# Softmax with a relative-position bias: the sixth row of chunk 0 loaded in sixteen uneven transfers, and a small bias load

## The chip, the cores and the metric

The kernel runs on one core of one Trainium2 chip. The metric is the device time of one execution in microseconds (us); the time given is the median of several runs. The core has five instruction engines (here VectorE = DVE, ScalarE = ACT, GpSimd = POOL and SyncE = SP are used) and 16 DMA engines that move data between HBM and the on-chip memory SBUF, which has 128 partitions. The trace of one profiled execution gives the start and length of each instruction and of each DMA packet.

## The reference

The input `logits` has the shape (2, 8, 2112, 2112) in float32, `rel_bias` (8, 33). To each row of logits a bias is added that depends on the head and on the clipped distance between the row's and the column's position, and a softmax is taken over the row.

```python
rel = pos[:, None] - pos[None, :]
rel_clipped = np.clip(rel, -max_rel, max_rel) + max_rel   # max_rel = 16
bias = rel_bias[:, rel_clipped].copy()
logits = logits + bias[None, :, :, :]
logits = logits - logits.max(axis=-1, keepdims=True)
exp = np.exp(logits)
return (exp / exp.sum(axis=-1, keepdims=True)).astype(np.float32)
```

285.5 MB are read and as many written.

## The kernel before

**Tiling.** The 2 x 8 x 2112 rows are divided among 128 partitions, 264 (`ROWS`) consecutive rows for each; 8 (`PB`) partitions make one head of one batch entry. A row is 2112 (`S`) floats, 8448 B. A chunk is R = 6 rows of every partition (6336 KB), N = 44 chunks in all, and four buffers `X[0]` to `X[3]` (`NBUF`) hold four chunks; STEP = 24 rows are one turn of the loops. Every chunk is loaded into a buffer, worked on there and stored from it.

**Engines.** For each chunk, DVE adds the bias and takes the negated maximum of each row (`add`, L166), ACT takes the exponential and its sum (`exps`, L175), DVE takes the reciprocal and multiplies (`scale`, L183 and L187). The bias of the rows lies as a strip `F`, which DVE copies once in 24 rows (`strip`, L160) out of a table `M` in PSUM. That table is made once ahead of the loop from `rel_bias` (L117 to L156): masks from two iotas of POOL, then the 33 values of the partition's own head picked from a copy of all 8 x 33 values (L131, L135), and then the table.

**Queues.** SP issues all loads and stores of logits and output, in program order. Ahead of its loop it issues chunk 0 as six transfers of one row each (L87 to L90; the first five count on the semaphore `pre`, the last on `ld[0]`), and then the loads of chunks 1 to 3 (L91, L92). In its loop it issues, in turn, the store of a finished chunk (which waits for the multiplies, semaphore `scaled`) and the load of the next chunk into a buffer whose store has landed (semaphore `st`). The last chunk is stored in two halves. The load of `rel_bias` is issued from ACT's queue (L97 to L100): it gives each of the 128 partitions a copy of all 264 values. DVE waits for it at L129, for five rows of chunk 0 at L190 (and then copies the first strip), and for the sixth row in the first `add`.

A transfer over all 128 partitions is divided among the 16 DMA engines, eight partitions for each, and each partition's piece is a packet.

Of the kernel before, what the change touches and what calls it, by code (L numbers as in the profile page):

```python
# [15 lines left out]
def kernel(  # L16
# [6 lines left out]
    nc = tc.nc  # L23
    P = 128
    B, H, S, S2 = logits.shape
    assert S == S2
    MR = 16
    W = 2 * MR + 1
    ROWS = B * H * S // P
    PB = S // ROWS  # L30
    assert ROWS * P == B * H * S and PB * ROWS == S and PB == H == 8
    R = 6
    NBUF = 4
# [4 lines left out]
    MW = S + ROWS - 1  # L38
    FW = S + STEP - 1
    BIG = 3.0e38  # L40

    io = ctx.enter_context(tc.tile_pool(name="io", bufs=1))
    X = [io.tile([P, R * S], FP32, tag=f"X{b}", name=f"X{b}") for b in range(NBUF)]
    F = io.tile([P, FW], FP32, tag="F", name="F")
    rbS = io.tile([P, W], FP32, tag="rbS", name="rbS")
# [3 lines left out]
    ip = io.tile([P, 3, PB], I32, tag="ip", name="ip")  # L49
# [3 lines left out]
    def view(t, offset, dims):  # L53

        return bass.AP(tensor=t.tensor, offset=t.offset + offset, ap=[[list(t.ap[0])[0], P]] + dims)

    def rows(t, j, n):

        return bass.AP(tensor=t.tensor, offset=t.offset + j * S, ap=[[ROWS * S, P], [1, n * S]])

    with tc.tile_critical(no_gpsimd_drain=True):
        ld = [nc.alloc_semaphore(f"ld{b}") for b in range(NBUF)]
# [3 lines left out]
        scaled = nc.alloc_semaphore("scaled")  # L66
        inv = nc.alloc_semaphore("inv")
        rb = nc.alloc_semaphore("rb")
        pre = nc.alloc_semaphore("pre")
        idx = nc.alloc_semaphore("idx")  # L70
        dve = nc.alloc_semaphore("dve")

        def take(eng, sem, n):
            eng.wait_ge(sem, n).then_inc(sem, -n)  # L74


        def load(j, b):
            nc.sync.dma_start(out=X[b][:, :], in_=rows(logits, j, R)).then_inc(ld[b], 16)
# [5 lines left out]
            ).then_inc(st[b], 16)  # L84


        for r in range(R):  # L87
            nc.sync.dma_start(
                out=X[0][:, r * S : (r + 1) * S], in_=rows(logits, r, 1)
            ).then_inc(ld[0] if r == R - 1 else pre, 16)  # L90
        for n in range(1, NBUF):  # L91
            load(n * R, n)  # L92

        rbB = view(F, 0, [[1, H * W]])
        nc.scalar.dma_start(  # L97
            out=rbB,
            in_=bass.AP(tensor=rel_bias.tensor, offset=rel_bias.offset, ap=[[0, P], [1, H * W]]),
        ).then_inc(rb, 16)  # L100
        nc.gpsimd.iota(ip[:, 0], pattern=[[0, PB]], base=0, channel_multiplier=1).then_inc(idx, 1)
        nc.gpsimd.iota(ip[:, 2], pattern=[[1, PB]], base=0, channel_multiplier=0).then_inc(idx, 1)  # L102

        v = nc.vector
        done = [0]

        def then(ins):
            done[0] += 1
            ins.then_inc(dve, 1)

        def settle():
            v.wait_ge(dve, done[0])

        SC = H * W
        mask = [F[:, SC + i * PB : SC + (i + 1) * PB] for i in range(9)]
        dp, dh, eq, hm, gt, le, lt, ra, rz = mask
        v.wait_ge(idx, 2)  # L117
        then(v.tensor_scalar(out=ip[:, 1], in0=ip[:, 0], scalar1=3, scalar2=7,  # L118
                             op0=ALU.logical_shift_right, op1=ALU.bitwise_and))
# [7 lines left out]
        for m, op in ((eq, ALU.is_equal), (gt, ALU.is_gt), (le, ALU.is_le), (lt, ALU.is_lt)):  # L127
# [4 lines left out]
            out=view(F, 0, [[W, H], [1, W]]), in0=view(F, 0, [[W, H], [1, W]]),  # L132
            in1=view(F, SC + 3 * PB, [[1, H], [0, W]]), op=ALU.mult))
        settle()
        then(v.tensor_reduce(out=rbS[:, :], in_=view(F, 0, [[1, W], [W, H]]),  # L135
                             axis=mybir.AxisListType.X, op=ALU.add))
        settle()
        low, high = rbS[:, W - 1 : W], rbS[:, 0:1]
        then(v.tensor_scalar(out=ra, in0=gt, scalar1=low, scalar2=None, op0=ALU.mult))  # L139
        then(v.tensor_scalar(out=rz, in0=gt, scalar1=low, scalar2=None, op0=ALU.mult))  # L140
        then(v.tensor_tensor(  # L141
            out=view(F, 0, [[W, PB], [1, W]]), in0=view(F, SC + 2 * PB, [[1, PB], [0, W]]),
            in1=view(rbS, W - 1, [[0, PB], [-1, W]]), op=ALU.mult))
# [6 lines left out]
            out=view(M, U, [[ROWS, PB], [1, W]]), in0=view(F, 0, [[W, PB], [1, W]]),  # L150
            in1=view(F, SC + 8 * PB, [[1, PB], [0, W]]), op=ALU.add))
        then(v.tensor_copy(out=view(M, U + W, [[ROWS, PB], [1, ROWS - W]]),  # L152
                           in_=view(F, SC + 7 * PB, [[1, PB], [0, ROWS - W]])))
        then(v.tensor_copy(out=M[:, 0:U], in_=low.to_broadcast([P, U])))  # L154
# [7 lines left out]
        def add(b):  # L162
            take(v, ld[b], 16)
            for r in range(b * R, (b + 1) * R):
                x = X[b][:, (r - b * R) * S : (r - b * R + 1) * S]
                v.tensor_tensor_reduce(  # L166
                    out=x, in0=x, in1=F[:, STEP - 1 - r : STEP - 1 - r + S], scale=-1.0, scalar=BIG,
                    op0=ALU.add, op1=ALU.min, accum_out=nmax[:, r : r + 1],
# [18 lines left out]
                    v.tensor_scalar_mul(out=x, in0=x, scalar1=rec[:, r : r + 1]).then_inc(scaled, 1)  # L187

        v.sem_inc(dve, -done[0])
        take(v, pre, 16 * (R - 1))  # L190
        with nc.Fori(0, ROWS - STEP + 1, STEP, engines=[ENG.DVE]) as j:  # L191
            strip(j)
            take(v, dve, 1)
# [51 lines left out]
```

## Time and profile before

| | |
|---|---|
| median of 3 runs | 1330.1 us (1329.99 to 1332.06) |
| span of the profiled execution, first to last instruction | 1327.7 us |
| DMA rate over the span | 430 GB/s |
| SP's DMA queue, share of 16 engines | 99.6% |
| busy: DVE, ACT, POOL | 74%, 43%, 0% |
| last multiply of DVE ends | 1303.6 us |

In the views of the profile, a row of the timeline gives start, length, engine, line, operation and tiles; in brackets stands how long the engine was idle before it and what ended that. `SPq` and `ACTq` are the instruction queues of SP and ACT, which issue DMAs. A row of the windows gives a stretch of time, its length, the busy time of DVE, ACT and POOL with the number of instructions, the clock of the matrix engine (which is not used here), the mean busy share of the 16 DMA engines and the rate in GB/s; a packet is counted whole in the window in which it starts, so a short window can show a share above 1. A row for a DMA queue gives packets, MB, and the share of the time of 16 engines.

### The profile page before, as it was taken

How to read it: one execution, taken by the hardware profiler on the slowest of the kernel's cores; microseconds unless marked ns; L12 is line 12 of the kernel's file. 1: busy time of each engine (PE TensorE's matmuls, PEld its weight loads, DVE VectorE, ACT ScalarE, POOL GpSimd, SP SyncE). 2: the span in 40 equal slices, each digit the busy share in tenths (PEclk: the TensorE clock that was granted, in tenths of full speed). 3: DMA queues.
4: the chain of work that ended last, by engine and by line, in shares of the span. 5: the costliest groups of instructions: out<-in, count | busy, mean ns of one | idle time of the engine just before them, and what ended most of it. 6: DMA issues, size and time to landing. Idle time of an engine off the chain costs nothing. (4 is left out here: it accounts for less than half of the span.)

```text
span 1327.7 us, 2454 instructions
## 1 busy us (share of the span) xinstructions
DVE 976.6 (74%) x911; ACT 575.2 (43%) x539; POOL 0.4 (0%) x6
## 2 busy tenths in 40 slices
DVE  6999667777777776687778777677877776687772
ACT  2564333444444343345444333444444343335440
POOL 0000000000000000000000000000000000000000
DMA  9999999999999999999999999999999999999998
GB/s 392 431 428 437 435 420 437 435 434 425 435 437 434 428 435 434 435 429 429 438 438 432 426 438 437 437 425 437 437 437 425 435 440 437 428 432 438 437 426 359
DMA packets 13683, 571.11 MB, mean 430 GB/s; under 512 B 1521, under 2 KB 1649, under 8 KB 1649
## 3 DMA queue, kind: packets, MB, share of 16 engines
q1 hardware_dynamic: 13536, 570.96, 99.6%
q10 hardware_dynamic: 144, 0.14, 0.1%
q14 instruction: 3, 0.02, 0.0%
HBM read 285.61 MB, written 285.47 MB: 430 GB/s over the span
## 5 line engine op out<-in xcount | busy, mean ns | idle before, releaser
L166 DVE CUSTOM_DVE_ANT_0 X<-X,F 128x2112 f32<-128x2112 f32 x264 | 605.2, 2354 | 301.3 <-DVEq L74 301.3
L175 ACT ACTIVATE X<-X,nmax 128x2112 f32<-128x2112 f32 x264 | 541.7, 2052 | 539.3 <-ACTq L74 517.6
L187 DVE TENSOR_SCALAR X<-X,rec 128x2112 f32<-128x2112 f32 x264 | 332.4, 1315 | 13.2
L175 ACT ACT_TABLE_LOAD x11 | 14.1, 1283 | 183.3 <-ACTq L74 183.3
L175 ACT ACTIVATION_READ_ACCUMULATOR X<-X,nmax 128x1 f32 x264 | 49.2, 186 | 0.0
L160 DVE COPY F<-M 128x2135 f32 x11 | 26.1, 2374 | 6.3 <-DVEq L74 6.3
L166 DVE DVE_READ_ACCUMULATOR2_ANT nmax<- 128x1 f32 x264 | 21.7, 82 | 0.0
L183 DVE RECIPROCAL rec<-tot 128x3 f32<-128x3 f32 x88 | 14.9, 170 | 0.0
L131 DVE TENSOR_TENSOR F<-F 128x264 f32<-128x264 f32 x1 | 0.4, 434 | 4.7 <-DMA F<-in_rel_bias_dram 4.7
L152 DVE COPY M<-F 128x1848 f32<-128x1848 f32 x1 | 2.1, 2077 | 0.0
L118 DVE TENSOR_SCALAR ip<-ip 128x8 int32<-128x8 int32 x1 | 0.2, 173 | 1.3 <-POOL ip L102 1.3
L135 DVE TENSOR_REDUCE rbS<-F 128x33 f32<-128x264 f32 x1 | 0.6, 610 | 0.0
L149 DVE TENSOR_TENSOR M<-F 128x264 f32<-128x264 f32 x1 | 0.4, 441 | 0.0
L141 DVE TENSOR_TENSOR F<-F,rbS 128x264 f32<-128x264 f32 x1 | 0.4, 425 | 0.0
L128 DVE TENSOR_SCALAR F<-F 128x8 f32<-128x8 f32 x4 | 0.4, 166 | 0.0
L154 DVE COPY M<-rbS 128x247 f32<-128x247 f32 x1 | 0.4, 408 | 0.0
L139 DVE TENSOR_SCALAR F<-F,rbS 128x8 f32<-128x8 f32 x1 | 0.2, 231 | 0.0
L145 DVE SCALAR_TENSOR_TENSOR F<-F,rbS 128x8 f32<-128x8 f32 x1 | 0.2, 225 | 0.0
L140 DVE TENSOR_SCALAR F<-F,rbS 128x8 f32<-128x8 f32 x1 | 0.2, 222 | 0.0
L146 DVE SCALAR_TENSOR_TENSOR F<-F,rbS 128x8 f32<-128x8 f32 x1 | 0.2, 219 | 0.0
L124 DVE TENSOR_TENSOR F<-ip 128x8 f32<-128x8 int32 x1 | 0.2, 167 | 0.0
L121 DVE TENSOR_TENSOR F<-ip 128x8 f32<-128x8 int32 x1 | 0.2, 166 | 0.0
(9 smaller groups left out, 1.2 us busy)
## 6 DMA issues: line engine op xcount, KB each, us to landing
X<-in_logits_dram SPq DMA_DIRECT2D x43, 6336.0 KB, 44.6
out_dram<-X SPq DMA_DIRECT2D x43, 6336.0 KB, 52.6
X<-in_logits_dram SPq DMA_DIRECT2D x6, 1056.0 KB, 12.1
out_dram<-X SPq DMA_DIRECT2D x2, 3168.0 KB, 21.1
F<-in_rel_bias_dram ACTq DMA_DIRECT2D x1, 132.0 KB, 6.2
```

What stands on the lines that cost most here:

```text
L128: then(v.tensor_scalar(out=m, in0=dp, scalar1=0.0, scalar2=None, op0=op))
L131: then(v.tensor_tensor(out=view(F, 0, [[W, H], [1, W]]), in0=view(F, 0, [[W, H], [1, W]]), in1=view(F, SC + 3 * PB, [[1, H], [0, W]]), op= ...
L135: then(v.tensor_reduce(out=rbS[:, :], in_=view(F, 0, [[1, W], [W, H]]), axis=mybir.AxisListType.X, op=ALU.add))
L141: then(v.tensor_tensor(out=view(F, 0, [[W, PB], [1, W]]), in0=view(F, SC + 2 * PB, [[1, PB], [0, W]]), in1=view(rbS, W - 1, [[0, PB], [-1, ...
L149: then(v.tensor_tensor(out=view(M, U, [[ROWS, PB], [1, W]]), in0=view(F, 0, [[W, PB], [1, W]]), in1=view(F, SC + 8 * PB, [[1, PB], [0, W]] ...
L152: then(v.tensor_copy(out=view(M, U + W, [[ROWS, PB], [1, ROWS - W]]), in_=view(F, SC + 7 * PB, [[1, PB], [0, ROWS - W]])))
L154: then(v.tensor_copy(out=M[:, 0:U], in_=low.to_broadcast([P, U])))
L160: v.tensor_copy(out=F[:, :], in_=M[:, bass.ds(ROWS - STEP - j, FW)]).then_inc(dve, 1)
L166: v.tensor_tensor_reduce(out=x, in0=x, in1=F[:, STEP - 1 - r : STEP - 1 - r + S], scale=-1.0, scalar=BIG, op0=ALU.add, op1=ALU.min, accum_ ...
L175: nc.scalar.activation(out=x, in_=x, func=EXP, scale=-1.0, bias=nmax[:, r : r + 1], accum_out=tot[:, r : r + 1],).then_inc(expd, 1)
L183: v.reciprocal(out=rec[:, r0 : r0 + HALF], in_=tot[:, r0 : r0 + HALF]).then_inc(inv, 1)
L187: v.tensor_scalar_mul(out=x, in0=x, scalar1=rec[:, r : r + 1]).then_inc(scaled, 1)
```

## The change

Three things change, all ahead of the loop.

*Chunk 0.* Its first five rows are one transfer over 128 partitions. The sixth row is cut into sixteen transfers (`FAN`). Each covers partitions that lie eight apart: for each `lane` from 0 to 7 one transfer of 15 - lane partitions (15, 14, down to 8), and then, for the lanes in reverse order, the remaining 1 + lane partitions of that lane (8, 7, down to 1). A transfer of k partitions is run by the k lowest DMA engines, one partition each, so that engine 0 takes 16 packets of 8448 B, engine 1 takes 15, and so on down to engine 7 with 9; engine 8 takes 7, and engine 15 none. Before, each engine took eight. The transfers count on two semaphores (`pre` and `fan`) in turn, and the last on `ld[0]`. SP issues all of them ahead of the loads of chunks 1 to 3.

*Bias load.* `rel_bias` goes to 16 partitions instead of 128, one for each group of eight. DVE clears the 264 columns first, and the load on ACT's queue waits for that.

*Spreading within a group.* After the 33 values are picked (now into a scratch area `RB` that was cleared before), DVE transposes the block in squares of 32 x 32, repeats every eighth column eight times, transposes back and copies the result to `rbS`: four instructions more.

```diff
+    GROUPS = P // 16
+    FAN = [(15 - lane, 0, lane) for lane in range(GROUPS)]
+    FAN += [(16 - k, k, lane) for k, _, lane in FAN[::-1]]
...
-        for r in range(R):
-            nc.sync.dma_start(
-                out=X[0][:, r * S : (r + 1) * S], in_=rows(logits, r, 1)
-            ).then_inc(ld[0] if r == R - 1 else pre, 16)
-        for n in range(1, NBUF):
-            load(n * R, n)
-        rbB = view(F, 0, [[1, H * W]])
-        nc.scalar.dma_start(
-            out=rbB,
-            in_=bass.AP(tensor=rel_bias.tensor, offset=rel_bias.offset, ap=[[0, P], [1, H * W]]),
-        ).then_inc(rb, 16)
...
+        then(v.memset(F[:, 0 : H * W], 0.0))
+        nc.scalar.wait_ge(dve, 1)
+        nc.scalar.dma_start(
+            out=bass.AP(tensor=F.tensor, offset=F.offset, ap=[[PB * list(F.ap[0])[0], P // PB], [1, H * W]]),
+            in_=bass.AP(
+                tensor=rel_bias.tensor, offset=rel_bias.offset, ap=[[0, P // PB], [1, H * W]]
+            ),
+        ).then_inc(rb, 16)
+        nc.sync.dma_start(
+            out=X[0][:, 0 : (R - 1) * S], in_=rows(logits, 0, R - 1)
+        ).then_inc(pre, 16)
+        PSX = list(X[0].ap[0])[0]
+        for i, (k, g, lane) in enumerate(FAN):
+            p = g * GROUPS + lane
+            nc.sync.dma_start(
+                out=bass.AP(
+                    tensor=X[0].tensor, offset=X[0].offset + p * PSX + (R - 1) * S,
+                    ap=[[GROUPS * PSX, k], [1, S]],
+                ),
+                in_=bass.AP(
+                    tensor=logits.tensor, offset=logits.offset + (p * ROWS + R - 1) * S,
+                    ap=[[GROUPS * ROWS * S, k], [1, S]],
+                ),
+            ).then_inc(ld[0] if i == len(FAN) - 1 else pre if i % 2 else fan, 16)
+        for n in range(1, NBUF):
+            load(n * R, n)
...
+        then(v.memset(F[:, RB : RB + 2 * Q], 0.0))
...
-        then(v.tensor_reduce(out=rbS[:, :], in_=view(F, 0, [[1, W], [W, H]]),
+        then(v.tensor_reduce(out=F[:, RB : RB + W], in_=view(F, 0, [[1, W], [W, H]]),
                              axis=mybir.AxisListType.X, op=ALU.add))
+        settle()
+        then(v.transpose(out=F[:, RT : RT + 2 * Q], in_=F[:, RB : RB + 2 * Q]))
+        settle()
+        then(v.tensor_copy(out=view(F, RC, [[Q, 2], [PB, Q // PB], [1, PB]]),
+                           in_=view(F, RT, [[Q, 2], [PB, Q // PB], [0, PB]])))
+        settle()
+        then(v.transpose(out=F[:, RW : RW + 2 * Q], in_=F[:, RC : RC + 2 * Q]))
+        settle()
+        then(v.tensor_copy(out=rbS[:, :], in_=F[:, RW : RW + W]))
...
-        take(v, pre, 16 * (R - 1))
+        take(v, pre, 16 * (len(FAN) // 2))
+        take(v, fan, 16 * (len(FAN) // 2))
```

More of the change, by code (lines that the diff above doesn't have):

```diff
@@ L40 @@
     BIG = 3.0e38
+    GROUPS = P // 16
+    FAN = [(15 - lane, 0, lane) for lane in range(GROUPS)]
+    FAN += [(16 - k, k, lane) for k, _, lane in FAN[::-1]]
+    assert sum(k for k, _, _ in FAN) == P
     io = ctx.enter_context(tc.tile_pool(name="io", bufs=1))
@@ L68 @@
         rb = nc.alloc_semaphore("rb")
-        pre = nc.alloc_semaphore("pre")
         idx = nc.alloc_semaphore("idx")
         dve = nc.alloc_semaphore("dve")
+        pre = nc.alloc_semaphore("pre")
+        fan = nc.alloc_semaphore("fan")
         def take(eng, sem, n):
@@ L84, in store @@
             ).then_inc(st[b], 16)
-        for r in range(R):
-            nc.sync.dma_start(
-                out=X[0][:, r * S : (r + 1) * S], in_=rows(logits, r, 1)
-            ).then_inc(ld[0] if r == R - 1 else pre, 16)
-        for n in range(1, NBUF):
-            load(n * R, n)
-        rbB = view(F, 0, [[1, H * W]])
-        nc.scalar.dma_start(
-            out=rbB,
-            in_=bass.AP(tensor=rel_bias.tensor, offset=rel_bias.offset, ap=[[0, P], [1, H * W]]),
-        ).then_inc(rb, 16)
-        nc.gpsimd.iota(ip[:, 0], pattern=[[0, PB]], base=0, channel_multiplier=1).then_inc(idx, 1)
-        nc.gpsimd.iota(ip[:, 2], pattern=[[1, PB]], base=0, channel_multiplier=0).then_inc(idx, 1)
         v = nc.vector
@@ L112, in settle @@
             v.wait_ge(dve, done[0])
+        then(v.memset(F[:, 0 : H * W], 0.0))
[24 more added lines that the diff above has]
+            load(n * R, n)
+        nc.gpsimd.iota(ip[:, 0], pattern=[[0, PB]], base=0, channel_multiplier=1).then_inc(idx, 1)
+        nc.gpsimd.iota(ip[:, 2], pattern=[[1, PB]], base=0, channel_multiplier=0).then_inc(idx, 1)
         SC = H * W
@@ L116 @@
         dp, dh, eq, hm, gt, le, lt, ra, rz = mask
+        Q = 32
+        RB, RT, RC, RW = [SC + 9 * PB + 2 * Q * i for i in range(4)]
+        then(v.memset(F[:, RB : RB + 2 * Q], 0.0))
         v.wait_ge(idx, 2)
```

## The prediction

> **What bounds the kernel now.** I read the page first (busy shares, DMA rows), then the chain of waits, the timeline of the start and of SP's queue, and last the DMA share and rate in short windows at both ends.
>
> ```profile
> span 1327.7 us, 2454 instructions
> DVE 976.6 (74%) x911; ACT 575.2 (43%) x539; POOL 0.4 (0%) x6
> GB/s 392 431 428 437 435 420 437 435 434 425 435 437 434 428 435 434 435 429 429 438 438 432 426 438 437 437 425 437 437 437 425 435 440 437 428 432 438 437 426 359
> q1 hardware_dynamic: 13536, 570.96, 99.6%
> ```
> ```profile
> 1301.05 2.54 DVE X L187 x2
> ```
>
> No engine of the core is full, but the DMA queue of SP holds all sixteen DMA engines 99.6% of the span. Only the first and the last of the forty slices fall clearly below the common 425 to 440 GB/s. The chain of waits ends with a multiply at 1303.6 us; the other 24 us are stores. So the end is the end of the last DMA engine's list of packets, and one engine's rate is 433 / 16 = 27.1 GB/s: 0.311 us for a row of 8448 B, 1.87 us for six, 0.94 us for three (the last stores).
>
> ```profile
> 19.50:20.00 0.50, 0.50 (x1) 0.00 (x0) 0.00 (x0) 1.00 2.36 1014
> 20.00:20.50 0.50, 0.50 (x1) 0.00 (x0) 0.00 (x0) 1.00 0.71 304
> 20.50:21.00 0.50, 0.36 (x1) 0.00 (x0) 0.00 (x0) 1.00 0.00 0
> ```
> ```profile
> 1320.00:1321.00 1.00, 0.00 (x0) 0.00 (x0) 0.00 (x0) 1.00 0.53 228
> 1321.00:1322.00 1.00, 0.00 (x0) 0.00 (x0) 0.00 (x0) 1.00 0.47 203
> 1322.00:1323.00 1.00, 0.00 (x0) 0.00 (x0) 0.00 (x0) 1.00 0.41 177
> 1323.00:1324.00 1.00, 0.00 (x0) 0.00 (x0) 0.00 (x0) 1.00 0.41 177
> 1324.00:1325.00 1.00, 0.00 (x0) 0.00 (x0) 0.00 (x0) 1.00 0.18 76
> 1325.00:1326.00 1.00, 0.00 (x0) 0.00 (x0) 0.00 (x0) 1.00 0.12 51
> 1326.00:1327.00 1.00, 0.00 (x0) 0.00 (x0) 0.00 (x0) 1.00 0.00 0
> ```
>
> These windows book a packet at its start (hence 1014 GB/s). When chunk 1 begins, the engines start together: out of a packet's 1.87 us, half a microsecond holds no start, so all starts lie within 1.4 us. At the end they are far apart. In 1320 to 1321 there start 228 KB / 25.3 KB = 9 packets, so about seven engines are on their last one, which ends near **1320.6**. In 1325 to 1326 two packets start (51 / 25.3), in the first half of it by the finer window, and end near **1326.2**:
>
> ```profile
> 1325.00:1325.50 0.50, 0.00 (x0) 0.00 (x0) 0.00 (x0) 1.00 0.24 101
> 1325.50:1326.00 0.50, 0.00 (x0) 0.00 (x0) 0.00 (x0) 1.00 0.00 0
> ```
>
> The six rates add to 912 KB, 912 / 433 = 2.1 us of all engines; with half a packet already running (0.47) the mean engine ends at 1322.6, 2.0 after the first, and the last 3.6 after the mean. The lists hold equal bytes, so some engines drifted up to 5.6 us behind over the run. The profile does not number the engines. A perfect division would be worth 3.6 us; one that loads the wrong engine costs its packets one for one, since no engine waits for another inside the stream.
>
> **The change part by part.** *Small bias load.* 128 packets of 1056 B become 16.
>
> ```profile
> 2.00:3.00 1.00, 0.43 (x5) 0.00 (x0) 0.00 (x0) 1.00 1.10 176
> 3.00:4.00 1.00, 0.00 (x0) 0.00 (x0) 0.00 (x0) 1.00 0.64 159
> 4.00:5.00 1.00, 0.00 (x0) 0.00 (x0) 0.00 (x0) 1.00 0.80 239
> 5.00:6.00 1.00, 0.00 (x0) 0.00 (x0) 0.00 (x0) 1.00 0.94 321
> 6.00:7.00 1.00, 0.00 (x0) 0.00 (x0) 0.00 (x0) 1.00 0.94 377
> 7.00:8.00 1.00, 0.81 (x2) 0.00 (x0) 0.00 (x0) 1.00 0.98 414
> ```
> ```profile
> q10 hardware_dynamic: 144, 0.14, 2.9%
> ```
>
> The second row is the bias queue within the first 25 us: 2.9% is 0.73 us of every engine. Its bytes alone would be 132 / 433 = 0.3 us; the whole ramp lacks 257 + 274 + 194 + 112 + 56 + 19 KB against 433 GB/s, 2.1 us. So the gain lies between 0.3 and 2.1. I take **0.7**, the row of the queue itself; the rest may be the first packets' latency, which stays.
>
> *Five rows in one transfer.* The same bytes on the same engines; large packets run no faster than the later slices' 437 against 433. Nothing, at most 0.1.
>
> *DVE and ACT before the loop.* Two memsets, two transposes, two copies are added, and the bias load now waits on ACT for the first memset; nothing else stands in ACT's queue before 23.65.
>
> ```profile
> 7.16 0.43 DVE L131 TENSOR_TENSOR F<-F 128x264 f32<-128x264 f32 x1 [4.69 <-DMA F<-in_rel_bias_dram]
> 12.06 0.17 DVE L155 COPY M<-rbS 128x16 f32<-128x16 f32 x1
> 18.48 2.38 DVE L160 COPY F<-M 128x2135 f32 x1 [6.26 <-DVEq L74]
> 21.17 2.36 DVE L166 CUSTOM_DVE_ANT_0 X<-X,F 128x2112 f32<-128x2112 f32 x1 [0.31 <-DVEq L74]
> 23.65 1.28 ACT L175 ACT_TABLE_LOAD   x1 [23.65 <-ACTq L74]
> ```
>
> All six instructions are narrower than the 0.43 us one (at most 264 columns): under 2.6 us between them. The bias may land later by one large row packet (five rows, 1.56 us). Both fit in DVE's 6.26 us of idling for chunk 0. Without this cover the loop starts later by what is missing, and then the next cover counts:
>
> ```profile
> 43.07 22.23 SPq L82 DMA_DIRECT2D out_dram<-X  x2
> ```
> ```profile
> 64.93 0.36 SPq L82 DMA_DIRECT2D out_dram<-X  x1
> ```
> ```profile
> 81.12 0.36 SPq L78 DMA_DIRECT2D X<-in_logits_dram  x1
> ```
>
> Store 1 is issued at 64.93 and is needed by the engines when store 0 has ended, which releases the load at 81.1: 16 us of room for a late sixth row (strip copy and adds wait for it). Beyond 16 us a delay would cost one for one.
>
> *SP's queue.* Six issues become seventeen ahead of chunk 1's load.
>
> ```profile
> 0.97 3.34 SPq L88 DMA_DIRECT2D X<-in_logits_dram  x6
> 4.36 1.74 SPq L78 DMA_DIRECT2D X<-in_logits_dram  x3
> ```
>
> At 3.34 / 6 = 0.56 us the loads of chunks 1 to 3 are issued from 0.97 + 17 x 0.56 = 10.5. Engine 15 needs them after five rows, 8 x 1.56 = 12.5 us from a start between 2.0 and 4.4, so from 14.5 on. Hidden, with 4 us over. Three waits for landings (two new sums, and the last transfer) replace two; each is passed when the last engine is done.
>
> *Sixteen packets on engine 0.* Engine 0 gets 8 packets more: 8 x 0.311 = **+2.5**; engine 15 gets 2.5 less, the ones between in steps of a packet. New is also where an engine writes. Every transfer in this trace gives each engine the same eight partitions; in the fan, engine i of a transfer goes on to a partition eight further on than engine i - 1, mostly another's. If 27.1 GB/s is the engine's own, that costs 0. If it belongs to the place in SBUF, two engines at one place halve each other: 16 x 0.311 = **+5.0** more for engine 0. The starts lie within 1.4 us, so engines of one transfer run side by side and the price is nearly all or nothing. I take 5.0. The nearest row is the ramp, where packets meet in disorder: at 4 to 5 us a share of 0.80 moves 239 GB/s, 299 per full share, so packets take 433 / 299 = 1.45 times their time. This shows that one engine's rate is not its own under all company; as a price by itself it would be 2.2.
>
> [...]
>
> *Sum.* An engine without drift ends at 1320.6; engine 0 then ends at 1320.6 - 0.7 + 2.5 + 5.0 = 1327.4, and with the mean engine's drift of 2.0 at 1329.4. The last one ended at 1326.2: **+3.2 us**. The span goes from 1327.7 to 1330.9. The median of the runs stands 2.4 above the profiled span, so I forecast 1330.1 + 3.2 = **1333.3 us**. With drift from 0 to 5.6 and the ramp's bounds its own range is 1330 to 1337.
>
> **The rivals.**
>
> *Own rate, and the spread ends the drift.* The engines leave the fan 16 x 0.311 = 5.0 us apart, about the 5.6 they reach by themselves. If what makes them drift is that they run in step, it stops, and engine 0 ends at 1320.6 - 0.7 + 2.5 + 0.4 of its own start = 1322.8, 3.4 earlier: **1326.7**. For it: the half-empty last windows. Against it: it needs nearly no drift in engine 0, when seven of sixteen lag at 1322 to 1324 (share 0.41). It decides if a fan packet takes no longer than 0.33 us.
>
> *The last two are in the middle.* If the two last engines have middle numbers, their lists hardly change: 1326.2 - 0.7 + 0.3 = 1325.8, so **1329.7**, no change. For it: exactly two engines in the last window. [...] The trace has two last engines but no numbers.
>
> *The late ones have low numbers, own rate.* 1326.2 - 0.7 + 2.5 = 1328.0: **1331.9**.
>
> *SP's queue fills.* The trace never shows more than nine loads pending. If a tenth waits for the first landing near 17 us, the remaining nine issues end near 22, and chunk 1 starts 3 us late on all engines: 1326.2 - 0.7 + 3 = 1328.5, **1332.4** or more.
>
> **How the numbers follow.** A measurement of this kernel tells about 0.2% from no change, 2.7 us: faster is below 1327.4, slower above 1332.8. The forecast has 0.52 (0.44 slower, 0.08 the same: less drift, a better ramp); own rate and no drift 0.21 (0.19 faster, 0.02 same); the middle 0.18 (0.16 same, 0.02 faster); low numbers 0.06 (0.04 same, 0.02 slower); SP 0.03 slower. Faster 0.21, same 0.30, slower 0.49. The range goes from the rival at 1326.7, rounded down to 1326.5, up to the forecast with full drift, 1337.
>
> **What would show it.** In windows of the first 35 us: a DMA share near 1 with a rate well under 433 GB/s while the sixth row loads means sharing (at twice the time for a packet, about half); 433 there means own rate. The first add (21.17 now) should come 8 to 10 us later with sharing, about 2 with own rate. SP's issue of chunk 1 near 10.5 refutes the full queue. The ramp should lack 0.7 us less, and store 1 still be issued before store 0 ends. At the end, one or two engines should run alone for several us after the others; if instead the share falls steadily over 5 us and the end comes near 1323, the first rival is right. I am wrong altogether if the last engine ends before 1326.2 with a sixth row that took long.

## The result and the profile after

The changed kernel takes **1334.0 us**, the median of 13 runs (1333.5 to 1334.3); the kernel before took 1330.3 in the runs made beside it (1329.4 to 1333.5). The ratio is 1.0025, with a 95% interval of 1.0017 to 1.0033: slower, by 3.6 us. The profiled execution took 1333.8 us with a span of 1332.0.

The page of the changed kernel, span and busy shares, rates in 40 slices, and the queue of SP:

```profile
span 1332.0 us, 2472 instructions
DVE 977.8 (73%) x917; ACT 575.2 (43%) x539; POOL 0.4 (0%) x6
GB/s 340 433 432 434 434 437 432 432 434 435 435 434 431 434 434 435 435 432 432 435 434 435 434 431 434 434 435 437 431 432 435 434 435 434 431 435 432 435 437 320
q1 hardware_dynamic: 13072, 570.96, 99.5%
```

The queue still fills the span. The first slice fell from 392 to 340 GB/s, the last from 359 to 320. The start of the changed kernel in windows (stretch, length, busy DVE, ACT and POOL, clock, DMA share, GB/s, a packet booked at its start):

```profile
14.00:16.00 2.00, 0.43 (x3) 0.00 (x0) 0.00 (x0) 1.00 0.67 207
16.00:18.00 2.00, 0.00 (x0) 0.00 (x0) 0.00 (x0) 1.00 1.18 266
18.00:20.00 2.00, 0.00 (x0) 0.00 (x0) 0.00 (x0) 1.00 1.26 245
20.00:22.00 2.00, 0.00 (x0) 0.00 (x0) 0.00 (x0) 1.00 1.19 203
22.00:24.00 2.00, 0.00 (x0) 0.00 (x0) 0.00 (x0) 1.00 0.78 186
24.00:26.00 2.00, 0.00 (x0) 0.00 (x0) 0.00 (x0) 1.00 0.82 287
26.00:28.00 2.00, 1.64 (x1) 0.00 (x0) 0.00 (x0) 1.00 1.05 456
```

From 16 to 24 us the DMA engines are busy (shares 1.18 to 0.78, 1.10 on average) and move (266 + 245 + 203 + 186) / 4 = 225 GB/s, about half of 433. The trace does not number the engines; below, an engine's number stands for its count of fan packets (engine 0 is the one with sixteen, engine 15 the one with none). In the packets behind these windows, a fan packet of 8448 B takes 319 ns at first, mostly 620 to 640 from 16 to 20 us, twice the 311 of the full rate, and up to 915 to 933 after 20.5 us, three times; engines already in chunk 1 take 3.4 to 4.75 us for a packet of 1.87. That two engines and then three meet at one place is the author's estimate from these times: the trace does not record which partitions an engine writes. The timeline shows what waits for the sixth row:

```profile
1.40 0.58 ACTq L105 DMA_DIRECT2D F<-in_rel_bias_dram  x1
1.43 11.80 SPq L117 DMA_DIRECT2D X<-in_logits_dram  x16
...
8.36 0.43 DVE L153 TENSOR_TENSOR F<-F 128x264 f32<-128x264 f32 x1 [5.90 <-DMA F<-in_rel_bias_dram]
...
13.27 1.30 SPq L83 DMA_DIRECT2D X<-in_logits_dram  x3
...
14.27 0.17 DVE L186 COPY M<-rbS 128x16 f32<-128x16 f32 x1
...
26.36 2.38 DVE L191 COPY F<-M 128x2135 f32 x1 [11.93 <-DVEq L79]
...
29.06 2.36 DVE L197 CUSTOM_DVE_ANT_0 X<-X,F 128x2112 f32<-128x2112 f32 x1 [0.31 <-DVEq L79]
...
72.82 0.35 SPq L87 DMA_DIRECT2D out_dram<-X  x1
...
86.25 0.36 SPq L83 DMA_DIRECT2D X<-in_logits_dram  x1
```

By the landing records the sixth row is complete at 26.4 us where it was at 20.6, 5.8 later. The first add comes 7.9 later, because the strip copy ahead of it, which began in the kernel before when five rows were in (18.48), now waits for fifteen of the sixteen fan transfers too (26.36). And the end of the changed kernel in windows:

```profile
1321.00:1322.00 1.00, 0.00 (x0) 0.00 (x0) 0.00 (x0) 1.00 1.00 431
...
1323.00:1324.00 1.00, 0.00 (x0) 0.00 (x0) 0.00 (x0) 1.00 0.47 203
...
1325.00:1326.00 1.00, 0.00 (x0) 0.00 (x0) 0.00 (x0) 1.00 0.24 101
1326.00:1327.00 1.00, 0.00 (x0) 0.00 (x0) 0.00 (x0) 1.00 0.06 25
...
1329.00:1330.00 1.00, 0.00 (x0) 0.00 (x0) 0.00 (x0) 1.00 0.06 25
1330.00:1331.00 1.00, 0.00 (x0) 0.00 (x0) 0.00 (x0) 1.00 0.00 0
```

From 1326 to 1330 one packet of 25 KB starts per microsecond: one engine alone, for four microseconds.

The landing records of the trace say where each engine was. Each value is the time in us at which the first, the mean and the last of the sixteen engines had chunk 1 in SBUF, and its last store in DRAM; "stream" is the mean engine's time between the two. The lines e1 to e12 are the runs of the next section.

```
                 chunk 1 landed       last store landed          stream   last behind
                 first  mean  last    first    mean     last     (mean)   the mean
before           34.75 35.13 35.58    1320.94  1323.05  1326.56  1287.92  3.51
after            36.54 38.57 41.11    1322.52  1324.84  1330.43  1286.27  5.59
e1 small bias    33.32 33.51 33.77    1319.80  1322.42  1327.69  1288.91  5.27
e2 five rows     34.41 34.64 35.15    1320.54  1322.73  1326.82  1288.09  4.09
e3 no fan        33.09 33.33 33.72    1320.11  1322.80  1328.62  1289.47  5.82
e4 eight apart   35.61 35.90 36.34    1321.68  1323.80  1327.71  1287.90  3.91
e5 half fan      36.38 37.41 38.57    1322.65  1325.22  1328.97  1287.81  3.75
e6 wide bias     38.27 40.17 42.82    1324.16  1326.40  1331.63  1286.23  5.23
e7 four heavy    36.33 37.52 40.26    1322.29  1324.50  1329.16  1286.98  4.66
e8 adjacent      36.88 37.20 37.77    1323.19  1325.25  1328.19  1288.05  2.94
e9 own places    33.24 35.96 38.71    1319.10  1322.41  1329.23  1286.45  6.82
e10 four late    33.14 34.55 38.28    1319.82  1322.22  1327.80  1287.67  5.58
e11 two late     33.12 33.94 38.26    1319.75  1322.25  1328.90  1288.31  6.65
e12 ladder       33.23 34.75 38.21    1319.95  1321.89  1327.09  1287.14  5.20
```

Read the two first lines against each other. The last engine ends 3.87 us later, and that is three terms: the mean engine has chunk 1 **3.44 us later**; it then runs the stream in **1.65 us less**; and the last engine ends **2.08 us further** behind the mean.

The packets show where the stream column differs. A chunk's packet (six rows of a partition) takes 1.87 us; after the first 75 us, the number of those that take over 1.95 us, and their excess divided by 16 engines, is

```
before 94, 1.71 us    e2 99, 1.86    e5 109, 1.54   e10 43, 0.59    after 1, 0.02   e12 1, 0.01
e1     99, 2.12       e3 99, 2.31    e8  92, 1.78   e11 73, 1.18    e6    1, 0.02
                      e4 88, 1.64                   e7  53, 0.84    e9    4, 0.05
```

They lie around the end of each chunk's load and are what is called drift below. In e1, e3, e10, e11 and e12, and in no other run, sixteen or seventeen more packets that start at 60.7 to 62.7 us take 2.1 to 3.4 us; this stall costs the mean engine 0.6 us in e1 and 0.8 to 0.95 in the other four. 1286.25 us and these two terms give every line of the stream column within 0.15. What the stall is, no run tells.

### The profile page after: what moved, and what is told of

It is laid out like the page before. It is cut to its first block, busy times and chain, and to the rows that moved or that the text cites. A ratio compares the mean times of both kernels' runs of the same rounds, so it can differ in the third digit from the quotient of the medians.

```text
span 1332.0 us, 2472 instructions
## 1 busy us (share of the span) xinstructions
DVE 977.8 (73%) x917; ACT 575.2 (43%) x539; POOL 0.4 (0%) x6
```

## The experiments

Two questions were open. Is the late start the price of the place (engines that write into the partitions of others) or of small strided transfers as such? And why do the engines drift apart in one kernel and not in another? All diffs are against the changed kernel, but those of e10 and e11 against e3 and that of e12 against e10. Medians stand with their range and, as a ratio to the kernel before run beside them, the 95% interval.

**e1: the small bias load and its preparation alone**, the sixth row and the five before it in six one-row transfers as before.

```diff
-        nc.sync.dma_start(
-            out=X[0][:, 0 : (R - 1) * S], in_=rows(logits, 0, R - 1)
-        ).then_inc(pre, 16)
-        PSX = list(X[0].ap[0])[0]
-        for i, (k, g, lane) in enumerate(FAN):
...
+        for r in range(R):
+            nc.sync.dma_start(
+                out=X[0][:, r * S : (r + 1) * S], in_=rows(logits, r, 1)
+            ).then_inc(ld[0] if r == R - 1 else pre, 16)
```

> The small bias load alone (memset, 16 partitions, transposes), with the six one-row transfers of before. Theory A: the 128 bias packets held up the start of the stream; the five rows were in by 15.7 us with the change and 18.0 before, so without the 128 packets the sixth row lands near 18.5 instead of 20.6 and the time is 2 us less, 1328.3. Rival B: the earlier start came from the five rows in one transfer, so here the sixth row still lands at 20.2 to 20.6 and the time is 1329.8 to 1330.3.

Measured: 1331.8 us (1330.1 to 1333.3, 11 runs), 1.0007 [0.9998, 1.0015]. Both expectations missed. The mean engine has chunk 1 1.6 us earlier than before, twice the 0.7 that the prediction took. The time does not show it: 0.6 us go to the stall at 61 us and 0.4 to more drift, and the last engine ends 5.3 us behind the mean where it was 3.5.

**e2: five rows in one transfer alone**, the sixth in one transfer over 128 partitions, bias load of before.

```diff
         nc.sync.dma_start(
             out=X[0][:, 0 : (R - 1) * S], in_=rows(logits, 0, R - 1)
         ).then_inc(pre, 16)
...
-        for i, (k, g, lane) in enumerate(FAN):
...
+        nc.sync.dma_start(
+            out=X[0][:, (R - 1) * S : R * S], in_=rows(logits, R - 1, 1)
+        ).then_inc(ld[0], 16)
...
+        rbB = view(F, 0, [[1, H * W]])
+        nc.scalar.dma_start(
+            out=rbB,
+            in_=bass.AP(tensor=rel_bias.tensor, offset=rel_bias.offset, ap=[[0, P], [1, H * W]]),
+        ).then_inc(rb, 16)
...
```

> The five rows in one transfer alone, the sixth as one transfer over 128 partitions, with the bias load of before. Theory A: nothing, 1330.3, sixth row at 20.2 to 20.6. Rival B: 2 us less, 1328.3.

Measured: 1330.5 us (1328.8 to 1332.2, 11 runs), 1.0001 [0.9992, 1.0010]; chunk 1 0.5 us earlier. The larger packets hold up the bias, which shares the engines with them; the timeline of e2:

```profile
14.52 0.43 DVE L133 TENSOR_TENSOR F<-F 128x264 f32<-128x264 f32 x1 [12.06 <-DMA F<-in_rel_bias_dram]
20.18 2.38 DVE L162 COPY F<-M 128x2135 f32 x1 [0.59 <-DVEq L74]
```

The multiply of the bias comes at 14.52 where it came at 7.16. That uses up DVE's idle time before the strip copy (0.59 left of 6.26) and moves the copy by 1.7 us, which the 16 us of cover behind it take up: no cost that can be told.

**e3: the change without the fan**, the sixth row in one transfer over 128 partitions.

```diff
-        for i, (k, g, lane) in enumerate(FAN):
...
+        nc.sync.dma_start(
+            out=X[0][:, (R - 1) * S : R * S], in_=rows(logits, R - 1, 1)
+        ).then_inc(ld[0], 16)
```

> All of the change but the sixteen uneven transfers: the sixth row is one transfer over 128 partitions. Both theories of the start: row six lands near 18.3. Theory S (the fan's cost is engines that write into one place and divide its rate): without the fan no packet is shared, the engines start chunk 1 within 1.4 us, drift apart again to about 5.6 us by the end, and the time is 1330.3 - 2.0 = 1328.3, 5.6 below the changed kernel. Rival N (the fan costs little, the loss arises later): within 1 us of 1334.

Measured: 1331.3 us (1330.2 to 1332.8, 11 runs), 1.0005 [0.9996, 1.0014]. That is 3 us above what was expected. With 1334.0 for the whole change, the fan is what costs. e3 has the earliest start (33.33) and the slowest stream (1289.47): of its 1.8 us it gives back 0.9 to the stall at 61 us and 0.6 to more drift. In a window of e3 while the sixth row loads:

```profile
16.00:17.00 1.00, 0.35 (x1) 0.00 (x0) 0.00 (x0) 1.00 1.02 431
```

**e4: the sixth row in 8 transfers of 16 partitions eight apart**, 8 packets on every engine, so the fan's distance between partitions without its uneven counts. **e8: in 8 transfers of 16 adjacent partitions**, as many packets and transfers, at other partitions.

```diff
-        for i, (k, g, lane) in enumerate(FAN):
-            p = g * GROUPS + lane
+        for i in range(8):
+            p = i * 1
...
-                    ap=[[GROUPS * PSX, k], [1, S]],
+                    ap=[[8 * PSX, 16], [1, S]],
...
```
```diff
+            p = i * 16
...
+                    ap=[[1 * PSX, 16], [1, S]],
...
```

> The sixth row as eight transfers of 16 partitions that lie eight apart: every engine takes eight packets, no skew, but each engine writes away from its own partitions as in the fan. Theory S: packets of the sixth row take about 0.62 us, the row 5.0 instead of 2.5, all engines alike; then they start chunk 1 together and drift as before: 1328.3 + 2.5 = 1330.8. Rival K (what costs is the skew, packets beyond eight on the low engines): packets take 0.32, the row 2.5, the time is that of the kernel without the fan, 1328.3.

> The sixth row as eight transfers of 16 adjacent partitions: as many transfers and packets as with partitions eight apart, every engine eight packets, only the place of the writes differs. [...] Rival T (many small transfers cost time by themselves): 220 GB/s again and a row of 5 us.

Measured: e4 1331.7 us (1329.5 to 1334.3, 12 runs), 1.0010 [1.0002, 1.0019]; e8 1332.7 us (1331.1 to 1334.3, 10 runs), 1.0017 [1.0007, 1.0026]. The same bytes by the same engines in windows, e4 and then e8:

```profile
16.00:17.00 1.00, 0.00 (x0) 0.00 (x0) 0.00 (x0) 1.00 1.10 228
17.00:18.00 1.00, 0.00 (x0) 0.00 (x0) 0.00 (x0) 1.00 0.90 211
```
```profile
16.00:17.00 1.00, 0.00 (x0) 0.00 (x0) 0.00 (x0) 1.00 0.88 152
17.00:18.00 1.00, 0.00 (x0) 0.00 (x0) 0.00 (x0) 1.00 1.15 194
18.00:19.00 1.00, 0.00 (x0) 0.00 (x0) 0.00 (x0) 1.00 0.87 161
19.00:20.00 1.00, 0.00 (x0) 0.00 (x0) 0.00 (x0) 1.00 1.10 203
```

e4 moves 211 to 228 GB/s in these windows, about half of the 431 of e3, and e8 has 152 to 203, less than the rival's 220. The row takes 2.56 us in e3, 5.0 in e4 and 6.1 to 7 in e8. So small transfers as such do not set the rate: with counts, sizes and number of transfers equal, the adjacent partitions are slower than those eight apart. How many engines met at one place in e8 was not shown. In every run a packet's place in DRAM goes with its partition, so the runs do not tell by themselves on which side of the transfer the engines meet.

**e5: half of the fan**, four transfers over all engines and four cut into two (engine 0 has 12 packets, engine 15 has 4).

```diff
-    FAN = [(15 - lane, 0, lane) for lane in range(GROUPS)]
-    FAN += [(16 - k, k, lane) for k, _, lane in FAN[::-1]]
+    FAN = [(16, 0, lane) for lane in range(4, GROUPS)]
+    CUT = [(15 - 2 * lane, 0, lane) for lane in range(4)]
+    FAN += CUT + [(16 - k, k, lane) for k, _, lane in CUT[::-1]]
```

> The fan halved: four lanes as transfers of 16 partitions eight apart, four lanes cut into 15 + 1, 13 + 3, 11 + 5 and 9 + 7, so that engine 0 takes 12 packets, the middle ones 9, engine 15 four. Theory D (engines that start apart do not drift; one single engine falls behind steadily by 5 us wherever it stands, and it has a middle number): the spread at chunk 1 is near 3 us instead of 4.6, only the steady engine moves, it has two packets less and less company, and ends alone some 1.5 us earlier: 1332.5. Rival L (half the spread is not enough, the engines drift again): several engines are late at the end and the runs scatter over 3 us, about 1331.

Measured: 1332.6 us (1332.1 to 1333.1, 11 runs), 1.0014 [1.0005, 1.0023]. The engines leave chunk 1 2.2 us apart, and several drift on to 5.7 and 6.3 behind the first: this ladder does not end the drift. The time is the one expected with no drift (1332.5), by luck; the engines do what the rival said.

**e6: the fan with the wide bias load** and the preparation of before.

```diff
-        nc.scalar.wait_ge(dve, 1)
-        nc.scalar.dma_start(
...
+        rbB = view(F, 0, [[1, H * W]])
+        nc.scalar.dma_start(
+            out=rbB,
+            in_=bass.AP(tensor=rel_bias.tensor, offset=rel_bias.offset, ap=[[0, P], [1, H * W]]),
+        ).then_inc(rb, 16)
...
```

> The changed kernel with the bias load of before (128 packets, no memset, no transposes). In the kernels without the fan the small load started the stream 1.5 us earlier and the time did not follow, since the drift grew. Theory D: with the fan nothing drifts but the one steady engine, so a start that is 0.5 us later (as the five large rows over the wide load showed against the small load: 19.4 against 18.1, 1.3) shows in full: 1335.3, and all runs within 1 us. Rival L (the drift takes up such differences here too): 1334.0.

Measured: 1335.0 us (1334.8 to 1335.2, 6 runs), 1.0030 [1.0017, 1.0042]. It starts 1.6 us later than the changed kernel and its time is 1.1 us longer; its mean engine ends 1.6 later. A later start comes through to the mean engine's end in kernels that drift as well: against the kernel before, e4 has 0.8 at chunk 1 and 0.75 at the end, e8 2.1 and 2.2. The earlier one of e1 and e3 does not.

**e7: four heavy engines.** Engines 0 to 3 have 17 packets each, the others 5.

```diff
-    FAN = [(15 - lane, 0, lane) for lane in range(GROUPS)]
-    FAN += [(16 - k, k, lane) for k, _, lane in FAN[::-1]]
+    FAN = [(16, 0, lane) for lane in range(5)]
+    FAN += [(4, g, lane) for lane in range(5, GROUPS) for g in range(0, 16, 4)]
```

> Five lanes as transfers of 16 partitions eight apart, three lanes as twelve transfers of four: engines 0 to 3 take 17 packets, engines 4 to 15 five. Theory D: the steady engine is one of 4 to 15, starts early and is overtaken by nobody: after 5 us of falling behind it stands about where engines 0 to 3 stand without falling behind; the time is near 1331, and the end is not one engine alone for 4 us. Rival P (an engine falls behind steadily because it starts late): one of the heavy engines loses 5 us and the time is 1335 or more.

Measured: 1332.6 us (1331.3 to 1334.2, 11 runs), 1.0013 [1.0004, 1.0022], 1.6 above what was expected. The four heavy engines begin 3.8 to 3.9 us behind and end 5.8 to 6.9 behind. Two of the light ones fall back too, from under 0.8 to 4.2 and 4.4, so one of them can be the steadily slow engine, but here it cannot be told from drift. That no heavy list makes an engine slow is seen in the kernel before, where the lists are equal and one engine falls back about 4 us in an even slope.

**e9: own places at first.** Sixteen transfers of 8 partitions four apart: engines 0 to 7 have 16 packets, 8 to 15 none.

```diff
-    GROUPS = P // 16
-    FAN = [(15 - lane, 0, lane) for lane in range(GROUPS)]
-    FAN += [(16 - k, k, lane) for k, _, lane in FAN[::-1]]
+    GROUPS = 4
+    FAN = [(8, block, lane) for block in range(0, P // 4, 8) for lane in range(4)]
```

> The sixth row as sixteen transfers of 8 partitions four apart, all on engines 0 to 7, sixteen packets each, engines 8 to 15 none. The first eight transfers write where engines 0 to 7 write in the large transfers too, the last eight where engines 8 to 15 write. Theory S: the first eight packets take 0.32 us each beside full-rate packets of chunk 1 on engines 8 to 15, so from 16 to 18 us the rate stays near 430; then both halves slow down to half, near 220, for some 5 us. Rival T: the small transfers are slow from the first on.

Measured: 1332.7 us (1332.5 to 1332.8, 10 runs), 1.0016 [1.0007, 1.0026]. Windows of e9:

```profile
15.00:16.00 1.00, 0.00 (x0) 0.00 (x0) 0.00 (x0) 1.00 1.40 575
16.00:17.00 1.00, 0.00 (x0) 0.00 (x0) 0.00 (x0) 1.00 0.49 203
17.00:18.00 1.00, 0.00 (x0) 0.00 (x0) 0.00 (x0) 1.00 1.87 625
18.00:19.00 1.00, 0.00 (x0) 0.00 (x0) 0.00 (x0) 1.00 0.56 144
19.00:20.00 1.00, 0.00 (x0) 0.00 (x0) 0.00 (x0) 1.00 1.44 313
20.00:21.00 1.00, 0.00 (x0) 0.00 (x0) 0.00 (x0) 1.00 1.33 296
21.00:22.00 1.00, 0.00 (x0) 0.00 (x0) 0.00 (x0) 1.00 0.62 127
```

Between 15 and 18 us (partitions 0 to 63) a packet takes 319 ns and the eight engines and their neighbours move (575 + 203 + 625) / 3 = 468 GB/s (a packet is booked at its start); from 18 to 22 (partitions 64 to 127, by the expectation the places of engines 8 to 15) it takes 628 to 655 ns and the rate is (144 + 313 + 296 + 127) / 4 = 220. Same engines, transfers of the same form, half the rate: that the place is another engine's there is read from these times. The two groups then run 5.1 us apart to the end. Each holds eight engines within 0.5 us of each other, and yet they hardly drift: one engine falls back 4.9 us in an even slope, the others less than 1, and the runs lie within 0.3 us. So engines in step do not always drift apart, and no ladder is needed to keep them from it.

**e10, e11: late engines at their own places.** To e3, 16 more rows for engines 0 to 3 (e10) or 0 and 1 (e11) alone, at the partitions where e9 has 319 ns a packet for these engines: rows of chunk 3, which its own load writes again later. This adds bytes; what it takes out is the sharing.

```diff
+        for p in (0, 1, 2, 3, 32, 33, 34, 35):
+            nc.sync.dma_start(
+                out=bass.AP(
+                    tensor=X[3].tensor, offset=X[3].offset + p * PSX,
+                    ap=[[4 * PSX, 4], [1, 2 * S]],
+                ),
...
+            ).then_inc(off, 16)
         for n in range(1, NBUF):
+            if n == 3:
+                take(nc.sync, off, 16 * 8)
             load(n * R, n)
```

> The kernel without the fan (small bias load, five rows, sixth row as one transfer of 128 partitions), and after it 16 more rows of 8448 B for each of engines 0 to 3 alone, each at that engine's own place, 16 x 0.311 = 5.0 us (rows of chunk 3 that its own load writes again later; loads of chunk 1 and 2 follow at once). If a spread of 5 us is what ends the drift and the place is what the fan paid for: four engines start chunk 1 5.0 us after the other twelve, nobody's packets double, the mean engine has chunk 1 at 33.3 + 1.25 = 34.6 and runs the stream in 1286.3 as in the kernels without drift (not 1287.9 to 1289.5), the last engine ends some 3.5 after the mean, at 1324.4, 2.2 us before the kernel before: about 1328.1 us, runs within 1 us of each other, faster than before. If the drift goes on whatever the spread, the four end 5 us or more behind a stream as slow as before: 1332 or more.

> The same with engines 0 and 1 alone late by 5.0 us. If it is the last engine's distance that ends the drift, two late ones do as well as four: mean start 33.3 + 0.6 = 33.9, stream 1286.3, last about 4 behind the mean, 1324.3 in the trace and about 1328 us. If each late engine only shelters the engines that it is apart from, the fourteen others, in step, drift among themselves as before: a stream of 1288 or more, 1330 to 1332 us, runs 3 us apart.

Measured: e10 1331.6 us (1330.6 to 1332.5, 11 runs), 1.0012 [1.0003, 1.0021]; e11 1332.8 us (1331.6 to 1333.7, 11 runs), 1.0018 [1.0009, 1.0027]. The starts came as forecast (mean 34.55 and 33.94), without sharing. The rest did not: the theory that a spread of 5 us by itself ends the drift falls. Lags behind the first engine, sorted, in the landing records of one transfer each:

```
e10   33 us  0.0 0.0 0.0 0.2 0.2 0.2 0.2 0.2 0.2 0.3 0.3 0.5 5.0 5.0 5.1 5.1
    1305 us  0.0 0.1 0.1 0.2 0.3 0.4 0.4 0.4 0.5 0.7 3.4 3.5 6.9 7.0 7.3 8.1
e11   33 us  0.0 0.0 0.0 0.1 0.1 0.1 0.2 0.2 0.2 0.2 0.3 0.4 0.5 0.5 5.1 5.1
    1305 us  0.0 0.0 0.1 0.2 0.2 0.3 0.4 0.4 0.4 0.5 3.3 4.0 4.1 6.1 8.9 9.2
after 37 us  0.0 0.1 0.5 0.6 0.6 1.0 1.4 1.5 2.3 2.7 3.1 3.1 3.4 3.7 4.0 4.6
    1307 us  0.0 0.1 0.4 0.5 0.6 1.0 1.4 1.5 2.2 2.7 3.1 3.7 4.3 4.5 4.6 8.0
```

The late group of e10 and e11 loses 2 to 4 us more, and some of the others fall back as well. The changed kernel keeps its ladder but for one engine and moves of up to 0.7 us in the first 200. In e9, where eight engines were set back by 5.1 us rather than four or two, the drift did end.

**e12: a ladder at own places.** As e10, but 16 more rows for engine 0, 14 for engine 1, down to 2 for engine 7.

```diff
-        for p in (0, 1, 2, 3, 32, 33, 34, 35):
+        for k, p in enumerate((0, 1, 2, 3, 32, 33, 34, 35), 1):
...
-                    ap=[[4 * PSX, 4], [1, 2 * S]],
+                    ap=[[4 * PSX, k], [1, 2 * S]],
...
```

> As with four engines late, but as a ladder: engine 0 gets 16 rows of 8448 B more, engine 1 14, and so on down to engine 7 with 2, each at its own place, so the engines start chunk 1 in steps of 0.62 us over 5.0 us and 8 to 15 together. If it is the ladder (no two engines of the spread in step) that ended the drift in the changed kernel, the mean engine has chunk 1 at 33.3 + 1.4 = 34.7 and runs the stream in 1286.3; only the steady slow engine, number 4 or 5 with 1.9 to 2.5 us of its own and 4.9 over the run, is behind: it ends at about 1326.4 in the trace, runs within 1 us, about 1330.2 us, no change. If what ended it was the fan's sharing at the start, or only a spread among all sixteen, the engines drift on as with four or two late: a stream of 1287.7 or more, the late ones 7 us or more behind, runs 2 us apart, 1331.5 to 1333 us.

Measured: **1330.3 us** (1330.2 to 1330.5, 11 runs), 0.9994 [0.9985, 1.0003], as the ladder would have it, and the runs lie within 0.3 us where those of before, beside it, lie within 5. Its lags and its end:

```
e12   33 us  0.0 0.0 0.0 0.1 0.1 0.2 0.3 0.5 0.8 1.4 2.0 2.5 3.3 3.7 4.4 5.0
     378 us  0.0 0.0 0.1 0.2 0.2 0.3 0.3 0.5 0.6 1.6 2.5 3.7 3.9 4.2 4.8 4.9
    1305 us  0.0 0.0 0.1 0.2 0.2 0.3 0.3 0.5 0.6 1.6 2.4 4.0 4.2 4.8 4.9 7.1
```
```profile
1322.00:1323.00 1.00, 0.00 (x0) 0.00 (x0) 0.00 (x0) 1.00 0.29 127
1323.00:1324.00 1.00, 0.00 (x0) 0.00 (x0) 0.00 (x0) 1.00 0.18 76
1324.00:1325.00 1.00, 0.00 (x0) 0.00 (x0) 0.00 (x0) 1.00 0.06 25
1325.00:1326.00 1.00, 0.00 (x0) 0.00 (x0) 0.00 (x0) 1.00 0.06 25
1326.00:1327.00 1.00, 0.00 (x0) 0.00 (x0) 0.00 (x0) 1.00 0.00 0
```

After small moves in the first 378 us the ladder stands still, and one engine slopes from 2.5 to 7.1; it is alone at the end. It began with the lag nearest to engine 4's 8 rows (8 x 0.311 = 2.5). The stream is 1287.14, 0.8 more than expected; the stall at 61 us (0.9) accounts for it, and after it one packet in the whole stream is slow. But e12 does not show that the steps of the ladder did this: it also sets back eight engines where e10 has four, and in e9 eight in step did as well.

No kernel tried beats the one before by more than its interval. What e12 suggests, a ladder in which the steadily slow engine comes first, was not tried.

## Why the prediction was right

The forecast of 1333.3 us was 0.7 low, and slower by over 0.2% was the likeliest outcome named. Its mechanism, two engines at one place halving each other, is the reading that fits e3 against e4 (431 GB/s and 211 to 228) and the two halves of e9 (319 ns a packet and 628 to 655). That the number came so close is luck: the engine that ends last is not the one that the sum follows, and the terms that were wrong cancelled. By the steps:

- **Small bias load, 0.7 us.** Mis-sized: 1.6 in e1 and, with the five rows, 1.8 in e3 (chunk 1 at 33.33 instead of 35.13). The row of the bias queue priced its bytes and packets; the missing 2.1 us of the whole ramp, the upper bound, was nearer. In the changed kernel the last packets of the first five rows end at 15.1 to 15.8 us on the sixteen engines, where they ended at 16.8 to 17.6.
- **Five rows in one transfer, nothing.** Holds (e2, 1.0001). The delay of the bias, put at 1.56 us, is 1.2 with the small load (8.36 for 7.16) and 7.4 with the old one.
- **DVE and ACT before the loop, hidden.** Holds: the new steps end at 14.4 us and DVE then waits 11.93 for the sixth row.
- **First add 8 to 10 us later.** Measured 7.9 (29.06 for 21.17), but 5.8 of it is the row; the rest is the strip copy, which the step did not have waiting for the fan. The cover of 16 us behind it held as well: store 1 is issued at 72.82, 13.4 before the load that store 0 releases at 86.25.
- **SP's queue.** An issue of the fan takes 11.80 / 16 = 0.74 us, not 0.56, so chunk 1's load is issued at 13.3, not 10.5. It is hidden but for 0.25 us on one engine, and not with 4 us over: one engine ends its five rows at 15.74, has no fan packet, and starts chunk 1 at 15.99. The rival with the full queue is refuted.
- **Engine 0's packets, +2.5 and +5.0.** Right in size: its sixth row lasts from 15.1 to 25.4 us, 10.2 where 2.5 would be usual, 7.7 more. The all-or-nothing choice of twice the time was right (mostly 620 to 640 ns where the full rate has 311); 1.45 times, read off the ramp, would have been too low. But the step took it as engine 0's alone. Others lose as well: engine 15, without a fan packet, still has chunk 1 3.4 us later than the first engine of e3 (36.54 for 33.09). In the forecast it would have gained 2.5. The spread at chunk 1 is 4.6 us and not the 10 that the step implies.
- **Drift of 2.0 us on engine 0.** This step failed. The engine at the foot of the ladder does not drift: the lag there is 4.6 us at 37 and at 1307 us, and it ends near 1327.0, close to the sum without drift (1327.4). Instead another engine, number 4 or 5 by its count of fan packets, fell from 3.1 to 8.0 and ends alone at 1330.4. Neither its 3.1 us from the fan nor its 4.9 us of slowness is a term of the sum. The rival's notion that a spread ends the drift was right for this kernel (in e10 and e11 a spread of 5 us did not), while its other half, own rate, was wrong: both happened together.
- **The last two in the middle.** The engine that ends last has a middle number (it has 11 or 12 fan packets), though it is only one, and the time did not stay.

What the fan's places cost can be read from e12, a ladder of nearly the same length (5.0 us) without sharing: its mean engine has chunk 1 at 34.75 instead of 38.57, 3.8 us earlier, and the time is 1330.3 instead of 1334.0, 3.65 less. Against the kernel before run beside each, it is 0.9994 for 1.0025. The sharing accounts for about the whole loss, though e12 even loads 72 rows more, which cost the mean engine 72 x 0.311 / 16 = 1.4 us.

## What to carry to other kernels

When one saturated DMA queue sets the end, ask of every transfer not only how many packets each engine gets but which partitions each engine writes: the sixth row moved at 431 GB/s in one transfer over all 128 partitions (e3), at 211 to 228 in transfers of 16 eight apart (e4) and at 152 to 203 in transfers of 16 adjacent ones (e8), and the fan cost an engine without a fan packet 3.4 us as well. Here a late start came through to the end (e8: 2.1 us at chunk 1, 2.2 at the end), while an early one was lost in part to drift and to a stall (e3: 1.8 and 0.25); so compare the landing times of all engines, not the time alone. Equal lists don't end together here (5.6 us apart in the kernel before), and runs that agree within 0.3 to 0.8 us, where most others scatter over 2 to 5, went with a stream without drift (e5, within 1.0 us, drifts).

## What the runs showed of the hardware

- **Places.** In e9 a packet of 8448 B took the same eight engines 319 ns at partitions 0 to 63 and 628 to 655 at 64 to 127; in the changed kernel it took 319 at first and up to 915 to 933 later. That two and three engines shared a place is the author's estimate from these times.
- **Engines with equal lists drift apart, in some kernels.** From starts within 0.8 us, six engines of the kernel before fall 3.2 to 5.6 us behind in the first 900 us or so and then stay there. Sixteen engines spread over 4.6 us (changed kernel, e6), eight spread over 5.0 us beside eight in step (e12) and two groups of eight 5.1 us apart (e9) hold nearly still; two or four engines set 5 us back (e10, e11) and sixteen spread over 2.2 us (e5) do not. In the kernel before, the lost time comes in 94 packets of 1.95 to 2.7 us where the stream turns from loads to stores; why an engine loses there, and what decides whether it does, was not settled.
- **A stall.** In the five kernels e1, e3 and e10 to e12 sixteen or seventeen packets at 61 us take 2.1 to 3.4 us rather than 1.87. Its cause is open.
- **One engine is steadily slower.** In the kernel before, the changed one, e6, e9 and e12 one engine loses 4 to 5 us in an even slope, about 0.4% of its time, or 50 ns per transfer of 15 us. Before, it was hidden behind the drifters. Why it is slower is open.
- **Issues.** A fan transfer of 15 to 1 partitions took SP 0.74 us to issue in the mean (0.43 to 1.03), one over 128 partitions 0.33 to 0.71 in the kernel before and the changed one.
